# Modulation sums of a two-layer encoder: from float32 products to float32r halves

## The chip, the cores and the metric

The kernel runs on one core of one Trainium2 chip. The metric is the device time of one execution in microseconds (us). The engines are named as in the profile: PE is TensorE (matrix products), PEld its weight loads, DVE is VectorE, ACT is ScalarE, POOL is GpSimd, SP is SyncE, whose queue here issues nearly all transfers.

## The reference

Two layers over 256 positions of width 2048. In each, a vector c gives six modulation vectors of 2048; the mixers' bodies are left out here.

```python
c_act = jax.nn.silu(c)
for l in range(DEPTH):
    mod = (c_act @ w_mod[l] + b_mod[l]).reshape(bn, 6, d)
    shift_m, scale_m, gate_m = mod[:, 0, None], mod[:, 1, None], mod[:, 2, None]
    shift_f, scale_f, gate_f = mod[:, 3, None], mod[:, 4, None], mod[:, 5, None]

    h = layer_norm(x) * (1.0 + scale_m) + shift_m
    proj = h @ w_in[l]
    ...
    y = jnp.concatenate([y_a, y_b, y_c, y_d], axis=-1) @ w_out[l]
    x = layer_norm(ALPHA * x + (1.0 + gate_m) * y, post_mix_g[l], post_mix_b[l])

    h = layer_norm(x) * (1.0 + scale_f) + shift_f
    y = conv_ffn(h, ffn_w_up[l], ffn_w_conv[l], ffn_b_conv[l], ffn_w_down[l])
    x = layer_norm(ALPHA * x + (1.0 + gate_f) * y, post_ffn_g[l], post_ffn_b[l])
return x
```

## The kernel before

Most products are float32r products of halves. A weight tile `wraw` (128x2048) is loaded by SP's queue and split in two pieces of 128x1024 (`weights`, L368): ACT casts the high half `whi` (L403), DVE subtracts it from the raw tile for the low half `wlo` (L404). The activations are split in the same way (`split`, L420). TensorE sums high by high, high by low and low by high. The pool `splitp` holds four `whi` and four `wlo` tiles; each is taken again when the products that read it are done. In the first stages of layer 0 the weights are used as plain float32 (`wexact`, L379); these tiles come from the same pool.

The modulation vectors are made beside all this by `mod_stream` (L265). For each of the sixteen row blocks of `w_mod` it loads a tile `wmod`, and DVE adds it, times that block's entry of silu(c), to an accumulator `macc` of 128x2048 (L211). What is left is the sum over the 128 partitions. `settle` (L258) does that when the next vector is under way:

- `gate_rows` (L244) is for the two gates of a layer. They are needed along the free axis, the same in every partition: `ones` (128x128) is the stationary operand, 512 columns of `macc` the moving one, in float32, four times. ACT evicts each (`gate`, L251). The bias was added to one row of `macc` before.
- `mod_cols` (L190) is for shift and scale, which are needed along the partitions: for each block of 128 columns `macc` is the stationary operand and one column of `ones` the moving one, so there are sixteen products of one column, after one that puts the bias there. ACT evicts sixteen columns.

The order on each engine is made by a scheduler when the program is built; the source order and the pools' releases are what it starts from. `pump` (L321) spreads the steps of `mod_stream` over the units of weights. `out_proj` (L554) is the output projection (`o` in the profile) and the FFN's down projection (`d`). It goes over the columns in three chunks; at the end of each, `finish` multiplies the result by the gate row on DVE (`yg`, L586), adds it to the residual (`x`, L587) and takes statistics (L590): for the first chunk, of 1024 columns, four times three operations. `g_c` and `v_c` are the gate and value halves of the FFN's up projection, `C_c` is a float32 part of layer 0's input projection.

Of the kernel before, what the change touches and what calls it, by code (L numbers as in the profile page):

```python
# [7 lines left out]
F32 = mybir.dt.float32  # L8
F32R = mybir.dt.float32r
AF = mybir.ActivationFunctionType  # L10
ALU = mybir.AluOpType
AX = mybir.AxisListType

P = 128
# [4 lines left out]
KT = D // P  # L19
# [12 lines left out]
SHIFT_M, SCALE_M, GATE_M, SHIFT_F, SCALE_F, GATE_F = range(6)  # L32
# [22 lines left out]
def encoder_kernel(ctx: ExitStack, tc: tile.TileContext, A: dict, consts: bass.AP, out: bass.AP):  # L55
    nc = tc.nc
    pe, act, dve, pool = nc.tensor, nc.scalar, nc.vector, nc.gpsimd

    keep = ctx.enter_context(tc.tile_pool(name="keep", bufs=1))
    rawp = ctx.enter_context(tc.tile_pool(name="rawp", bufs=4))  # L60
    splitp = ctx.enter_context(tc.tile_pool(name="splitp", bufs=4))
# [11 lines left out]
    def tmp_tile(name):  # L73
        return tmpp.tile([P, 512], F32, tag="tmp", name=name)

    def ms_tile(name):
        return msp.tile([P, 512], F32, tag="ms", name=name)
# [4 lines left out]
    def mm(o, lhsT, rhs, start, stop):  # L82
        pe.matmul(o, lhsT, rhs, start=start, stop=stop, skip_group_check=True)  # L83

    def ident_act(o, i, scale, bias):
        return act.activation(out=o, in_=i, func=AF.Identity, scale=scale, bias=bias)
# [7 lines left out]
    ident = cst[:, 0:128]  # L94
# [2 lines left out]
    rotdup = cst[0:64, 384:512]  # L97
    cosT = cst[:, 512:768]
    sinT = cst[:, 768:1024]
    ones = keep.tile([P, P], F32, name="ones")  # L100
    pool.memset(ones, 1.0)
    mhalf = keep.tile([P, 4], F32, name="mhalf")
    pool.memset(mhalf, -0.5)

# [40 lines left out]
    bcol = []  # L145
# [40 lines left out]
    MOD, MOD_BY = {}, {}  # L186
# [3 lines left out]
    def mod_cols(l, m, k0, acc):  # L190

        n = acc.shape[1] // P
        ps = ms_tile("ps_mod")
        mm(ps[:, 0:n], ident, bcol[l][:, m * KT + k0 : m * KT + k0 + n], True, False)
        for j in range(n):
            mm(ps[:, j : j + 1], acc[:, j * P : (j + 1) * P], ones[:, 0:1], False, True)
        cols = keep.tile([P, n], F32, name=f"mod_{l}_{m}_{k0}")
        if m in (SHIFT_M, SHIFT_F):
            done = act.copy(cols, ps[:, 0:n])
        else:  # L200
            done = ident_act(cols, ps[:, 0:n], 1.0, ones[:, 0:1])
        for j in range(n):
            MOD[(l, m, k0 + j)] = cols[:, j : j + 1]
            MOD_BY[(l, m, k0 + j)] = done.ins.name

    def mod_step(acc, w, kt, first):
        col = cact[:, kt : kt + 1]
        if first:
            i = dve.tensor_scalar(out=acc, in0=w, scalar1=col, scalar2=None, op0=ALU.mult)
        else:  # L210
            i = dve.scalar_tensor_tensor(out=acc, in0=w, scalar=col, in1=acc, op0=ALU.mult, op1=ALU.add)  # L211
        held(i, "mod")

    def mod_piece(l, ms, k0, nkt):


        n, width = len(ms), nkt * P
        nk = 2048 // (n * width)
        acc = tmpp.tile([P, D], F32, tag="macc", name="qacc", bufs=2)[:, : n * width]
        units = []  # L220

        def unit(u):
            raw = raw_tile("wmod").rearrange("p (k m c) -> p k m c", k=nk, m=n)
            for i, m in enumerate(ms):
                c0 = m * D + k0 * P
                nc.sync.dma_start(
                    out=raw[:, :, i, :],
                    in_=A["w_mod"][l, u * nk * P : (u + 1) * nk * P, c0 : c0 + width].rearrange(
                        "(k p) c -> p k c", p=P
                    ),  # L230
                )
            for k in range(nk):
                mod_step(acc, raw[:, k, :, :].rearrange("p m c -> p (m c)"), u * nk + k, u == 0 and k == 0)

        for u in range(KT // nk):
            units.append(lambda u=u: unit(u))

        def sums():
            for i, m in enumerate(ms):
                mod_cols(l, m, k0, acc[:, i * width : (i + 1) * width])  # L240

        return units, sums

    def gate_rows(l, m, acc):  # L244

        g = keep.tile([P, D], F32, tag="gate", name=f"gate_{l}_{m}")
        for q in range(4):
            c = slice(q * 512, (q + 1) * 512)
            ps = ms_tile("ps_gate")
            mm(ps, ones, acc[:, c], True, True)  # L250
            ident_act(g[:, c], ps, 1.0, ones[:, 0:1])  # L251
        GATE[(l, m)] = g

    GATE = {}
# [3 lines left out]
    def settle(i=0):  # L258
        l, m, acc, k0, k1 = late.pop(i)
        if m in (GATE_M, GATE_F):  # L260
            gate_rows(l, m, acc)
        else:
            mod_cols(l, m, k0, acc[:, k0 * P : k1 * P])

    def mod_stream(order):  # L265
# [4 lines left out]
        for l, m in order:  # L270
            if (l, m) == (0, GATE_F):

                for u in range(4):
                    for v, acc in held_back.items():
                        raw = raw_tile("wmod").rearrange("p (k c) -> p k c", k=4)
                        nc.sync.dma_start(
                            out=raw,
                            in_=A["w_mod"][0, 4 * u * P : 4 * (u + 1) * P, v * D + LATE_KT * P : (v + 1) * D].rearrange(
                                "(k p) c -> p k c", p=P
                            ),  # L280
                        )
                        for k in range(4):
                            mod_step(acc[:, LATE_KT * P :], raw[:, k, :], 4 * u + k, u + k == 0)
                        if u == 3:
                            late.append((0, v, acc, LATE_KT, KT))
                        yield
            while len(late) >= 2:
                if late[0][:2] in WITH_NORM:
                    yield
                else:  # L290
                    settle()
# [5 lines left out]
            for kt in range(KT):  # L297
                raw = raw_tile("wmod")
                nc.sync.dma_start(out=raw[:, :w], in_=A["w_mod"][l, kt * P : (kt + 1) * P, m * D : m * D + w])
                if kt == KT - 1 and m in (GATE_M, GATE_F):  # L300
                    row = raw_tile("brow")
                    nc.sync.dma_start(out=row[0:1, :], in_=A["b_mod"][l : l + 1, m * D : (m + 1) * D])
                mod_step(acc[:, :w], raw[:, :w], kt, kt == 0)
                if kt == KT - 1:
                    if m in (GATE_M, GATE_F):
                        dve.tensor_tensor(out=acc[0:1, :], in0=acc[0:1, :], in1=row[0:1, :], op=ALU.add)
                    late.append((l, m, acc, 0, k1))
                yield
                if kt == 1 and late and late[0][:2] not in WITH_NORM:
                    settle()  # L310
# [16 lines left out]
    def need(l, m, k1=KT):  # L327
        while (l, m, k1 - 1) not in MOD and (l, m) not in GATE:
            at = [i for i, x in enumerate(late) if x[:2] == (l, m) and x[4] == k1]
            if at:  # L330
                settle(at[0])
            else:
                assert next(mods, "end") != "end"
# [25 lines left out]
    def held(i, kind):  # L359

        name, n = hold[kind]
        if n > 0:
            hold[kind][1] = n - 1
            tc.add_manual_dep(i.ins, name, order_dep, reason="the norm is what the next products wait for")
# [55 lines left out]
    def split(dst, src):  # L420
        hi, lo = dst[:2]
        act.copy(hi, src)  # L422
        dve.tensor_tensor(out=lo, in0=src, in1=hi.bitcast(F32), op=ALU.subtract)  # L423
# [970 lines left out]
def build(inputs):  # L1394
    import numpy as np
    import concourse.bacc as bacc

    nc = bacc.Bacc("TRN2", target_bir_lowering=False, num_devices=1)
    arrays, A = {}, {}
    for name in _INS:  # L1400
        a = np.ascontiguousarray(inputs[name])
        arrays[f"in_{name}_dram"] = a
        A[name] = nc.dram_tensor(f"in_{name}_dram", a.shape, mybir.dt.from_np(a.dtype), kind="ExternalInput").ap()
    c = _constants()
    arrays["in_consts_dram"] = c
    consts = nc.dram_tensor("in_consts_dram", c.shape, F32, kind="ExternalInput").ap()
    out = nc.dram_tensor("out_0_dram", (1, S, D), F32, kind="ExternalOutput").ap()
    with tile.TileContext(nc) as tc:
        encoder_kernel(tc, A, consts, out)
    return nc, arrays  # L1410
# [8 lines left out]
```

## Time and profile before

| what | value |
| --- | --- |
| three runs | 2348.81, 2357.82, 2362.06 us |
| median | 2357.82 us |
| span of the profiled execution | 2350.0 us |

For the profiled execution the page gives the span alone, no time of its own; the three runs are other executions. The span lies 1.2 us above the lowest of them and 7.8 below the median.

In the profile, a row such as "1525.44 3.87 PE L83 MATMUL ps_gate<-macc,ones ... x8" says that eight matmuls that began at line 83 started at 1525.44 us and were done 3.87 us later; L83 is the helper `mm`, so products are told apart by the names of their tiles. Matmuls are pipelined: their own lengths overlap, and what one costs in a stream is the distance of the starts.

### The profile page before, as it was taken

The page shows a single profiled execution, that of the slowest core. Times are in us where ns is not written, and L with a number is a line of the kernel's source. Part 1 is how long each engine was busy: PE and PEld are TensorE (multiplying, and loading weights), DVE is VectorE, ACT ScalarE, POOL GpSimd, SP SyncE. Part 2 cuts the span into 40 slices and gives each one's busy share as a digit, 9 for nine tenths or more (in the row PEclk, how much of TensorE's full clock was granted, in tenths as well). Part 3 has the DMA queues.
Part 4 walks back from the last instruction along what each step waited for, and adds up shares of the span by engine and source line. Part 5 has one row for each costly group of instructions (what it writes and reads, how often), then busy time and mean ns, then how long its engine had stood idle before and what let it go on. Part 6 is the DMA issues. An engine that isn't in the chain of part 4 may idle for free. (4 is left out here: it accounts for less than half of the span.)

```text
span 2350.0 us, 30996 instructions
## 1 busy us (share of the span) xinstructions
PE 2259.1 (96%) x12183; PEld 1924.6 (82%) x12183; DVE 1811.3 (77%) x2293; ACT 1036.4 (44%) x1478; POOL 38.0 (2%) x59
## 2 busy tenths in 40 slices
PE   6899999799999999999989999989999999999998
PEld 4688886498888888888878999867888888888786
DVE  6868987789888887988976986787676656665676
ACT  2221241345455544544535434435454455554553
POOL 2000000000000000000000000000000000000000
PEclk9899999899999999999998999999999999999999
DMA  9999779498889898898756566856767655556554
GB/s 338 368 316 329 285 274 383 159 341 309 308 312 329 291 327 296 309 328 294 274 186 228 191 227 199 297 185 233 236 234 247 205 190 181 193 183 197 179 197 144
DMA packets 226491, 605.17 MB, mean 258 GB/s; under 512 B 14484, under 2 KB 27012, under 8 KB 208676
## 3 DMA queue, kind: packets, MB, share of 16 engines
q1 hardware_dynamic: 225560, 602.29, 73.2%
q8 instruction: 95, 1.56, 0.3%
q0 software_dynamic: 784, 0.90, 0.1%
q14 instruction: 52, 0.43, 0.0%
HBM read 601.05 MB, written 2.10 MB: 257 GB/s over the span
## 5 line engine op out<-in xcount | busy, mean ns | idle before, releaser
L404 DVE TENSOR_TENSOR wlo<-wraw,whi 128x1024 fp32r<-128x1024 f32 (+1 forms) x645 | 775.7, 1216 | 360.4 <-ACT whi L403 354.5
L403 ACT CAST whi<-wraw 128x1024 fp32r<-128x1024 f32 (+1 forms) x645 | 670.9, 1046 | 817.8 <-PE g_c L83 208.2
L83 PE MATMUL v_c<-hT,whi 128*128 128x512 f32 x1344 | 473.1, 397 | 0.0
L83 PE MATMUL g_c<-hT,whi 128*128 128x512 f32 x1272 | 450.3, 398 | 0.0
L83 PE MATMUL d<-whi,a 128*128 128x512 f32 x1344 | 388.4, 391 | 0.3 <-ACT whi L403 0.3
L211 DVE SCALAR_TENSOR_TENSOR macc<-wmod,cact,macc 128x2048 f32<-128x2048 f32 (+2 forms) x180 | 358.1, 1993 | 38.9 <-DMA wmod<-in_w_mod_dram 38.2
L83 PE MATMUL v_c<-hT,wlo 128*128 128x256 f32 x1344 | 376.9, 281 | 0.0
L83 PE MATMUL g_c<-hT,wlo 128*128 128x256 f32 x1272 | 358.2, 282 | 0.0
L83 PEld LDWEIGHTS v_c<-hT,whi 128*128 128x128 f32 x1344 | 252.3, 188 | 60.1
L83 PEld LDWEIGHTS d<-whi,a 128*128 128x128 f32 x1344 | 252.9, 188 | 53.7 <-ACT whi L403 0.8
L83 PEld LDWEIGHTS g_c<-hT,whi 128*128 128x128 f32 x1272 | 239.7, 188 | 57.4 <-issue 0.5
L83 PEld LDWEIGHTS v_c<-hT,wlo 128*128 128x128 f32 x1344 | 254.0, 189 | 0.3 <-DVE wlo L404 0.2
L83 PEld LDWEIGHTS g_c<-hT,wlo 128*128 128x128 f32 x1272 | 241.4, 190 | 0.7 <-issue 0.5
L83 PE MATMUL d<-wlo,a 128*128 128x512 f32 x672 | 234.4, 391 | 0.8 <-DVE wlo L404 0.8
L83 PEld LDWEIGHTS d<-wlo,a 128*128 128x128 f32 x672 | 126.6, 188 | 27.6 <-DVE wlo L404 1.1
L83 PE MATMUL o<-whi,a 128*128 128x512 f32 x352 | 99.6, 392 | 0.1
L708 DVE SCALAR_TENSOR_TENSOR convD<-gluD,pm,convD 128x245 f32<-128x245 f32 (+23 forms) x240 | 98.7, 467 | 0.5
L423 DVE TENSOR_TENSOR a<-g,a 128x512 fp32r<-128x512 f32 x132 | 89.0, 686 | 0.0
L83 PE MATMUL D_c<-hT,whi 128*128 128x256 f32 x432 | 83.9, 294 | 2.5 <-ACT hT L422 2.0
L422 ACT CAST a<-g 128x512 fp32r<-128x512 f32 x132 | 81.3, 616 | 7.2 <-PE d L83 6.0
L211 DVE SCALAR_TENSOR_TENSOR qacc<-wmod,cact,qacc 128x1024 f32<-128x1024 f32 (+1 forms) x75 | 80.3, 1070 | 2.6 <-DMA wmod<-in_w_mod_dram 0.5
L83 PEld LDWEIGHTS o<-whi,a 128*128 128x128 f32 x352 | 66.0, 188 | 14.4 <-ACT whi L403 0.5
(310 smaller groups left out, 2667.4 us busy)
## 6 DMA issues: line engine op xcount, KB each, us to landing
wraw<-in_ffn_w_up_dram SPq DMA_DIRECT2D x176, 1024.0 KB, 5.4
wmod<-in_w_mod_dram SPq DMA_DIRECT2D x136, 1024.0 KB, 5.7
wraw<-in_ffn_w_down_dram SPq DMA_DIRECT2D x88, 1024.0 KB, 5.2
wraw<-in_w_in_dram SPq DMA_DIRECT2D x34, 1024.0 KB, 5.9
wmod<-in_w_mod_dram SPq DMA_DIRECT2D x64, 512.0 KB, 8.0
wmod<-in_w_mod_dram SPq DMA_DIRECT2D x32, 768.0 KB, 6.8
wraw<-in_w_out_dram SPq DMA_DIRECT2D x24, 1024.0 KB, 7.3
wexact<-in_w_in_dram SPq DMA_DIRECT2D x44, 512.0 KB, 6.5
```

Of the source, the lines that this page charges most:

```text
L83: pe.matmul(o, lhsT, rhs, start=start, stop=stop, skip_group_check=True)
L211: i = dve.scalar_tensor_tensor(out=acc, in0=w, scalar=col, in1=acc, op0=ALU.mult, op1=ALU.add)
L403: act.copy(hi[:, :m], r)
L404: i = dve.tensor_tensor(out=lo[:, :m], in0=r, in1=hi[:, :m].bitcast(F32), op=ALU.subtract)
L422: act.copy(hi, src)
L423: dve.tensor_tensor(out=lo, in0=src, in1=hi.bitcast(F32), op=ALU.subtract)
L708: dve.scalar_tensor_tensor(out=yd[:, j, 30 - k :], in0=glu[:, j, : S - 30 + k], scalar=CW(k, j), in1=yd[:, j, 30 - k :], op0=ALU.mult, op1 ...
```

## The change

The sums over the partitions of six vectors (the gates of both layers, and layer 1's SHIFT_F and SCALE_F) are no longer float32 products. `macc` is split in halves first, `mhi` by a cast on ACT and `mlo` by a subtraction on DVE, in two pieces of 128x1024, whose tiles come from the ring of the weight halves. A gate is then eight float32r products, high and low for each of four blocks of 512 columns. For SHIFT_F and SCALE_F of layer 1 the new function `mod_rows` uses stationary operands of four columns, of which one is ones: so block j of 512 columns lands in row j of one PSUM bank. That is copied (`mrow`), turned by four transposes, and DVE adds the bias (and 1 for the scale). The other shifts and scales stay as they were. `ones` becomes a view of the new tile `onesR`, which is cast on ACT at the start.

```diff
-    ones = keep.tile([P, P], F32, name="ones")
-    pool.memset(ones, 1.0)
+    flat = tmp_tile("flat")
+    pool.memset(flat[:, 0:P], 1.0)
+    pool.memset(flat[:, P : P + 16], 0.0)
+    for j in range(4):
+        pool.memset(flat[:, P + 5 * j : P + 5 * j + 1], 1.0)
+    onesR = keep.tile([P, P + 16], F32R, name="onesR")
+    act.copy(onesR, flat[:, : P + 16])
+    ones = onesR[:, 0:P].bitcast(F32)
...
+    def halves(acc, c0):
+        hi = splitp.tile([P, 1024], F32R, tag="whi", name="mhi")
+        lo = splitp.tile([P, 1024], F32R, tag="wlo", name="mlo")
+        split((hi, lo), acc[:, c0 : c0 + 1024])
+        return [(hi[:, i * 512 : (i + 1) * 512], lo[:, i * 512 : (i + 1) * 512]) for i in range(2)]
+
+    def mod_rows(l, m, acc):
+
+        ps = ms_tile("ps_row")
+        for j, pair in enumerate(halves(acc, 0) + halves(acc, 1024)):
+            for n, part in enumerate(pair):
+                mm(ps[0:4, :], onesR[:, P + 4 * j : P + 4 * j + 4], part, j + n == 0, j + n == 4)
+        row = tmp_tile("mrow")
+        act.copy(row[0:4, :], ps[0:4, :])
+        ps = ms_tile("ps_mod")
+        for i in range(4):
+            pe.transpose(ps[:, 4 * i : 4 * i + 4], row[0:4, i * P : (i + 1) * P], ident[0:4, 0:4])
+        cols = keep.tile([P, KT], F32, name=f"mod_{l}_{m}")
+        done = dve.scalar_tensor_tensor(
+            out=cols.rearrange("p (i j) -> p i j", i=4),
+            in0=ps[:, 0:KT].rearrange("p (i j) -> p i j", i=4),
+            scalar=0.0 if m == SHIFT_F else 1.0,
+            in1=bcol[l][:, m * KT : (m + 1) * KT].rearrange("p (j i) -> p i j", i=4),
+            op0=ALU.add,
+            op1=ALU.add,
+        )
...
-        for q in range(4):
-            c = slice(q * 512, (q + 1) * 512)
-            ps = ms_tile("ps_gate")
-            mm(ps, ones, acc[:, c], True, True)
-            ident_act(g[:, c], ps, 1.0, ones[:, 0:1])
+        for h in range(2):
+            for i, (hi, lo) in enumerate(halves(acc, h * 1024)):
+                c0 = h * 1024 + i * 512
+                ps = ms_tile("ps_gate")
+                mm(ps, onesR[:, 0:P], hi, True, False)
+                mm(ps, onesR[:, 0:P], lo, False, True)
+                ident_act(g[:, c0 : c0 + 512], ps, 1.0, ones[:, 0:1])
...
+        elif (l, m) in ((1, SHIFT_F), (1, SCALE_F)):
+            mod_rows(l, m, acc)
```

How the orders differ is shown at three places. A row holds its number on that engine, the line of the program, the operation with its tiles, the shape, and how often it stands in a row.

VectorE at layer 1's GATE_F, in the FFN's down projection (`d`; `x_88` and `x_89`, later `x_95` and `x_96`, are the two halves of the residual; `a<-g,a` are low halves of activations). Before:

```order
1535 L404 TENSOR_TENSOR wlo<-wraw,whi 128x1024 x2
1536 L423 TENSOR_TENSOR a<-g,a 128x2x256
1537 L404 TENSOR_TENSOR wlo<-wraw,whi 128x1024 x2
1538 L586 TENSOR_TENSOR yg<-d_000_17175,gate_5_17983 128x512
1539 L586 TENSOR_TENSOR yg<-d_001_17176,gate_5_17983 128x512
1540 L587 SCALAR_TENSOR_TENSOR x_88<-x_88,yg 128x512 x2
1541 L590 BN_STATS st_d_17147<-x_88 128x6 x2
1542 L586 TENSOR_TENSOR yg<-d_010_17177,gate_5_17983 128x512
1543 L586 TENSOR_TENSOR yg<-d_011_17178,gate_5_17983 128x512
1544 L587 SCALAR_TENSOR_TENSOR x_89<-x_89,yg 128x512 x2
1545 L590 BN_STATS st_d_17148<-x_89 128x6 x2
1546 L404 TENSOR_TENSOR wlo<-wraw,whi 128x1024 x2
```

And now:

```order
1545 L464 TENSOR_TENSOR a<-g,a 128x2x256
1546 L464 TENSOR_TENSOR mlo<-macc,mhi 128x1024 x2
1547 L445 TENSOR_TENSOR wlo<-wraw,whi 128x1024
1548 L627 TENSOR_TENSOR yg<-d_000_17230,gate_5_18038 128x512
1549 L627 TENSOR_TENSOR yg<-d_001_17231,gate_5_18038 128x512
1550 L628 SCALAR_TENSOR_TENSOR x_95<-x_95,yg 128x512 x2
1551 L631 BN_STATS st_d_17202<-x_95 128x6 x2
1552 L627 TENSOR_TENSOR yg<-d_010_17232,gate_5_18038 128x512
1553 L627 TENSOR_TENSOR yg<-d_011_17233,gate_5_18038 128x512
1554 L628 SCALAR_TENSOR_TENSOR x_96<-x_96,yg 128x512 x2
1555 L631 BN_STATS st_d_17203<-x_96 128x6 x2
1556 L445 TENSOR_TENSOR wlo<-wraw,whi 128x1024 x4
```

Before, the pair of low halves of the next unit of weights stood ahead of the twelve residual operations. Now the two `mlo` and one `wlo` stand there, and the second `wlo` of that unit is the first of the four behind them.

TensorE at the same gate, from the end of the first chunk's products (`d_010`, `d_011`) into the second chunk (`d_102400`). Before:

```order
9328 L83 MATMUL d_010_17177<-whi,a 128x512
9329 L83 MATMUL d_011_17178<-whi,a 128x512
9330 L83 MATMUL ps_gate<-macc,ones 128x512 x3
9331 L83 MATMUL d_102400_18028<-whi,a 128x512
9332 L83 MATMUL ps_gate<-macc,ones 128x512
9333 L83 MATMUL d_102400_18028<-wlo,a 128x512
9334 L83 MATMUL d_102400_18028<-whi,a 128x512 x2
```

And now:

```order
9360 L83 MATMUL d_010_17232<-whi,a 128x512
9361 L83 MATMUL d_011_17233<-whi,a 128x512
9362 L83 MATMUL ps_gate<-mhi,onesR 128x512 x2
9363 L83 MATMUL d_102400_18095<-whi,a 128x512
9364 L83 MATMUL d_102400_18095<-wlo,a 128x512
9365 L83 MATMUL d_102400_18095<-whi,a 128x512
9366 L83 MATMUL ps_gate<-mlo,onesR 128x512 x2
9367 L83 MATMUL d_102400_18095<-whi,a 128x512
9368 L83 MATMUL d_102400_18095<-wlo,a 128x512
9369 L83 MATMUL d_102400_18095<-whi,a 128x512 x2
9370 L83 MATMUL d_102400_18095<-wlo,a 128x512
9371 L83 MATMUL ps_gate<-mhi,onesR 128x512
```

Four rows of float32 (each shown as two instructions in the profile) have become eight, with the high and low products of a block apart and products of the next chunk in between.

SyncE's queue ahead of layer 0's GATE_M, where the last float32 weights of the input projection (`wexact`) are loaded. Before:

```order
75 L381 DMA wexact<-in_w_in_dram 128x1024
76 L299 DMA wmod<-in_w_mod_dram 128x1536 x2
77 L381 DMA wexact<-in_w_in_dram 128x1024 x2
78 L299 DMA wmod<-in_w_mod_dram 128x1536 x2
79 L381 DMA wexact<-in_w_in_dram 128x1024 x2
80 L299 DMA wmod<-in_w_mod_dram 128x1536 x3
81 L381 DMA wexact<-in_w_in_dram 128x1024 x2
82 L389 DMA wraw<-in_w_out_dram 128x2x1024
```

And now:

```order
75 L422 DMA wexact<-in_w_in_dram 128x1024
76 L340 DMA wmod<-in_w_mod_dram 128x1536 x2
77 L422 DMA wexact<-in_w_in_dram 128x1024 x2
78 L340 DMA wmod<-in_w_mod_dram 128x1536 x5
79 L430 DMA wraw<-in_w_out_dram 128x2x1024
80 L340 DMA wmod<-in_w_mod_dram 128x1536 x2
81 L430 DMA wraw<-in_w_out_dram 128x2x1024
82 L422 DMA wexact<-in_w_in_dram 128x1024
83 L340 DMA wmod<-in_w_mod_dram 128x1536
84 L422 DMA wexact<-in_w_in_dram 128x1024 x3
85 L340 DMA wmod<-in_w_mod_dram 128x1536
```

The last four loads of `wexact` stood as one pair ahead of three `wmod` and a second pair behind them, both ahead of the output projection's first `wraw`. Now they stand behind the first two `wraw`: one, then a `wmod`, then three together.

More of the change, by code (lines that the diff above doesn't have):

```diff
@@ L204, in mod_cols @@
             MOD_BY[(l, m, k0 + j)] = done.ins.name
+    def halves(acc, c0):
[22 more added lines that the diff above has]
+        )
+        for k in range(KT):
+            at = 4 * (k % 4) + k // 4
+            MOD[(l, m, k)] = cols[:, at : at + 1]
+            MOD_BY[(l, m, k)] = done.ins.name
     def mod_step(acc, w, kt, first):
```

## The prediction

> **What bounds the kernel now.** I read the page first, then TensorE's waits, then the chain of waits, then the single stretches that the change touches.
>
> ```profile
> span 2350.0 us, 30996 instructions
> PE 2259.1 (96%) x12183; PEld 1924.6 (82%) x12183; DVE 1811.3 (77%) x2293; ACT 1036.4 (44%) x1478; POOL 38.0 (2%) x59
> PE   6899999799999999999989999989999999999998
> ```
>
> TensorE is busy for 96% of the span. The dips are at the start, in slice 8 and where a LayerNorm stands. VectorE is the next engine with 77%, so there is room on it on average, but not in every place.
>
> ```profile
> PE ps_xT L535 <- ACT xn L86: 36.5, 10, 7.8
> PE ps_xT L1241 <- ACT xn L86: 14.0, 2, 13.7
> PE D_c L83 <- DVE wlo L404: 3.4, 2, 2.6
> ```
>
> These are the longest waits of TensorE (total, number of times, longest). The first two are norms; the change does not touch them. In the streams of out projection and FFN, where five of the six changed sums stand, TensorE hardly waits at all. So there a microsecond taken from TensorE is a microsecond of the span, as long as the next weight halves arrive that much earlier too. That last condition decides this case.
>
> **The four gates.** What a gate costs now is seen in the chain (start, length, what), at layer 1's GATE_F:
>
> ```profile
> 2214.99 1.72 PE ps_gate L83 x4
> ...
> 2216.71 1.13 PE ps_gate L83 x2
> 2217.84 0.23 PE d L83
> 2218.07 0.87 PE ps_gate L83 x2
> 2218.93 9.09 PE d L83 x40
> ```
>
> Its eight instructions (each of the four float32 products shows as two) take 1.72 + 1.13 + 0.87 = 3.72 us. The last row has the price of a float32r product of 512 columns: 9.09 / 40 = 0.227 us. The new gate is eight of those, 1.81 us if it flows. So a gate frees **1.9 us** of TensorE. What it costs elsewhere are two casts on ScalarE and two subtractions on VectorE, of the same 128x1024 shape as the weight halves:
>
> ```profile
> L404 DVE TENSOR_TENSOR wlo<-wraw,whi 128x1024 fp32r<-128x1024 f32 (+1 forms) x645 | 775.7, 1216 | 360.4 <-ACT whi L403 354.5
> L403 ACT CAST whi<-wraw 128x1024 fp32r<-128x1024 f32 (+1 forms) x645 | 670.9, 1046 | 817.8 <-PE g_c L83 208.2
> ```
>
> That is 2.1 us of ScalarE and 2.4 us of VectorE for each sum. ScalarE waits 817.8 us for its inputs over the span, so its share is hidden. VectorE's is not hidden everywhere, so each gate is worked out at its place.
>
> Layer 1, GATE_M (first out projection chunk; start, length, what):
>
> ```profile
> 1525.44 3.87 PE L83 MATMUL ps_gate<-macc,ones 128*128 128x512 f32 x8
> 1526.43 1.22 DVE L404 TENSOR_TENSOR wlo<-wraw,whi 128x1024 fp32r<-128x1024 f32 x1
> 1527.56 1.28 DVE L586 TENSOR_TENSOR yg<-o,gate 128x512 f32<-128x512 f32 x2
> ...
> 1533.55 1.28 DVE L590 BATCH_NORM_STATS2 st_o<-x 128x6 f32<-128x512 f32 x2
> 1534.74 2.35 DVE L404 TENSOR_TENSOR wlo<-wraw,whi 128x1024 fp32r<-128x1024 f32 x2
> ```
>
> Twelve operations of the residual (yg, x, bn_stats) take 7.2 us on VectorE, from 1527.56 to 1534.74, and the next low half stands behind them. In the changed order mlo, mlo and one wlo come first, from 1526.43: three of 1.2 us end at 1530.0, the twelve end at 1537.2, and the second wlo (call it wlo b) at 1538.4. TensorE's product that reads wlo b is the 47th instruction from the gate's first one; 46 x 0.227 = 10.4 us after 1525.44, that is 1535.9. So TensorE would stand **2.5 us** for it: 1.9 won, 2.5 lost, +0.6 us.
>
> Layer 1, GATE_F (the same place of the FFN's down projection):
>
> ```profile
> 2213.66 1.06 ACT L403 CAST whi<-wraw 128x1024 fp32r<-128x1024 f32 x1 [2.51 <-PE d L83]
> 2214.74 2.58 DVE L404 TENSOR_TENSOR wlo<-wraw,whi 128x1024 fp32r<-128x1024 f32 x2 [2.25 <-ACT whi L403]
> 2217.24 1.28 DVE L586 TENSOR_TENSOR yg<-d,gate 128x512 f32<-128x512 f32 x2
> 2223.22 1.28 DVE L590 BATCH_NORM_STATS2 st_d<-x 128x6 f32<-128x512 f32 x2
> 2224.42 2.35 DVE L404 TENSOR_TENSOR wlo<-wraw,whi 128x1024 fp32r<-128x1024 f32 x2
> ```
>
> Here both wlo stand ahead of the twelve operations now; in the changed order the two mlo take their places, wlo a follows, and wlo b goes behind the twelve. VectorE is idle before 2214.74. The cast that stands at 2213.66 becomes the first mhi. From 2214.74 on: mlo to 2215.9, the second (its cast ends at 2216.1) to 2217.2, wlo a to 2218.4, the twelve (7.2 us) to 2225.6, wlo b to 2226.7. The gate starts at about 2214.8; wlo b is the 47th again, 10.4 us later, and some 0.4 us are lost inside the gate where its evictions wait behind a cast of ScalarE: 2225.6. A stand of 1.1 us: 1.9 - 0.4 - 1.1 = **0.4 us won**.
>
> Layer 0, GATE_F lies in an up projection without residual operations behind it:
>
> ```profile
> 653.34 2.92 PE L83 MATMUL ps_gate<-macc,ones 128*128 128x512 f32 x6
> ```
>
> The last two of its eight instructions come after two other products, and it costs the same 3.7 us. The low-half gate products are put about 14 instructions behind the high-half ones, 14 x 0.227 = 3.2 us, against 2.4 us of mlo. I count the whole **1.9 us**.
>
> Layer 0, GATE_M lies in the stage with plain float32 weights, which share the ring of tiles (L379) with the new halves:
>
> ```profile
> 284.84 2.06 SPq L381 DMA_DIRECT2D wexact<-in_w_in_dram  x2
> 295.03 2.06 SPq L381 DMA_DIRECT2D wexact<-in_w_in_dram  x2
> 306.66 3.79 PE L83 MATMUL ps_gate<-macc,ones 128*128 128x512 f32 x8
> 310.28 12.04 PE L83 MATMUL C_c<-hF,wexact 128*128 128x256 f32 x55
> wexact<-in_w_in_dram SPq DMA_DIRECT2D x44, 512.0 KB, 6.5
> ```
>
> The mhi and mlo take four of the eight tiles, so the last four loads of wexact on SyncE's queue, issued at 284.84 and 295.03 now, wait for products just ahead of the gate and for the gate itself: they issue at 306 to 309. With 6.5 us to landing that gives 312.5 to 315.5. TensorE reaches the first of them after a gate of 1.8 us and 16 C_c products of 12.04 / 55 = 0.219 us: 306.7 + 1.8 + 3.5 = 312. So it stands 0.5 to 3.5 us, less what a quicker landing gives back; I take 1.6 and 0.3 inside the gate, which leaves **0** (bounds -1.6 and +2).
>
> **The two sums of shift and scale.** Layer 1's SHIFT_F and SCALE_F now:
>
> ```profile
> 790.32 3.71 PE L83 MATMUL ps_mod<-ones,macc 128*128 128x1 f32 x32
> 921.55 0.29 PE L83 MATMUL ps_mod<-bcol,cst 128*128 128x16 f32 x2
> 921.69 3.76 PE L83 MATMUL ps_mod<-ones,macc 128*128 128x1 f32 x32
> 925.31 0.78 PE L83 MATMUL g_c<-hT,whi 128*128 128x512 f32 x1
> 926.10 0.63 PE L83 MATMUL g_c<-hT,whi 128*128 128x512 f32 x1
> 928.65 0.39 PE L83 MATMUL g_c<-hT,whi 128*128 128x512 f32 x1
> 279.64 0.38 PE L973 MATMUL ps_pT<-cst,p 128*128 128x128 f32 x2
> ```
>
> From 921.55 to 925.31 are 3.76 us for 34 instructions, and the other sum takes the same. In their place come eight products of 512 columns, 1.81 us, and four small transposes. No transpose of four rows is in the trace; the nearest are the ps_pT, two in 0.21 us by their starts, so 0.1 each. Below, they could cost next to nothing; above, 0.23 like a full product. I take 0.1, 0.4 in all: 2.2 us against 3.76. Waits for the first mhi or mrow I put at 0.3, since other products stand between mrow's copy and its transposes. So **1.2 us** each, 2.4 for both (bounds 0 and 3.5). The halves run beside up projections, with two wlo and a macc step per unit on VectorE; the bias addition and mrow's copy are one operation each, needed only at the norm at 1569.
>
> **The clock.** The rows from 925.31 show more: five pairs of g_c products (a whi and a wlo) take 3.34 us, up to 928.65. In a whole unit from the chain, the first row below, a pair takes 22.61 / 64 = 0.35 us, five 1.77. The windows (behind the busy times the granted clock, then DMA) name the reason:
>
> ```profile
> 1643.02 22.61 PE g_c L83 x128
> 795.00:800.00 5.00, 5.00 (x31) 4.43 (x30) 0.66 (x1) 1.40 (x2) 0.00 (x0) 1.00 0.85 311
> 920.00:925.00 5.00, 5.00 (x42) 4.80 (x41) 4.14 (x8) 2.65 (x4) 0.00 (x0) 1.00 0.58 203
> 925.00:930.00 5.00, 5.00 (x22) 4.34 (x22) 2.29 (x2) 0.28 (x1) 0.00 (x0) 0.66 0.96 317
> ```
>
> The clock was 0.66 on average just behind the narrow products, and the five pairs lost 3.34 - 1.77, about **1.5 us**. The same stretch at 790.32 was followed by none of this: 1.00 in the window from 795. With dense products in its place I expect that the drop at 925 goes.
>
> [...]
>
> **Start.** One small cast, one more table load and five more memsets stand ahead of the modulation vector. The first modulation step waits for its weights, so I count 0 (bounds 0 and 1.3).
>
> **The sum.** +0.6 - 0.4 - 1.9 + 0 - 2.4 - 1.5 + 0 = **-5.6 us**, -0.24%. It is made against the span of 2350.0 us; the runs were 2348.81 to 2362.06 with a median of 2357.82, and I take the difference to the median: **2352 us**. About 0.5% (11.8 us) is what a measurement of this kernel can tell from no change.
>
> **Rivals.**
>
> *All of it is won.* The waits that I put at the out projections and at wexact do not come about, because VectorE catches up: 4 x 1.9 + 2 x 1.5 + 1.5 = 12.1 us, 2345.7 us, -0.51%. For it: VectorE's 77%, and 46 products are a long cover. Against it: the order puts wlo b behind the twelve operations by name, and the row at 1534.74 shows that even now it ends at 1535.9, just when it is needed. Chance 0.15.
>
> *The halves hold up the ring.* The mechanism: mhi and mlo take two of four whi and two of four wlo tiles, so the unit of weights behind a sum can be cast only when the sum has read its halves. If at a sum a cast and a subtraction (1.05 + 1.22 = 2.27 us) come late for both tiles of that unit, TensorE stands 4.5 us: a gate then loses 2.6 us and a folded sum 3.0 (4.5 less 1.5). At all six, 4 x 2.6 + 2 x 3.0 = 16.4 us less the 1.5 of the clock: about +15, 2373 us. Half of it at all places, or all at three, is near +6. It decides where the first mhi is cast later than 2.3 us ahead of its first product. For it: the casts' idle time is mostly ended by TensorE's release (208.2 us of it by g_c). Against it: at 2213.66 the cast that becomes mhi ends before the gate starts. Chance 0.12.
>
> *The clock drops elsewhere.* The gates save, but a stretch of narrow or waiting work that escaped now is caught (a later modulation sum, or the stand for wlo b): 1.5 us back for each, two of them +3. Then about -3, 2355 us. Chance 0.13; inside "no change".
>
> **The numbers.** Forecast -5.6 and its neighbourhood (-1 to -10): 0.6. Faster by over 0.5%: the first rival, and a little of the forecast's edge: 0.17. Slower by over 0.5%: most of the second rival: 0.10. Within: 0.73. The range reaches from 2343 (the full gain, and a few us for the spread of the runs around their median) to 2363 (half of the ring's price).
>
> **What will show it.** ps_gate should be 32 products of about 0.39 us in the list by tile, ps_row 16, and their stretches near 2 us. wlo b behind the first twelve residual operations of each layer 1 projection should be named as what o and d wait for, 2.5 and 1.1 us. The loads of wexact should issue near 306. The window at 925 should show a clock of 1.00. I am wrong if TensorE waits for mhi, mlo or whi by more than a microsecond at the up projections, or if ScalarE's order delays something that I left out.

## The result and the profile after

The changed kernel took 2351.69 us (median of 22 runs, 2338.61 to 2357.93), the kernel before 2357.47 us beside it (22 runs, 2343.77 to 2363.85). The ratio is 0.9973 with a 95% interval of 0.9961 to 0.9986: 3 to 9 us faster. The median's 5.8 us lie beside the forecast 5.6, well inside what was called no change.

The two profiled executions say the opposite at first sight. The page of the changed kernel:

```profile
span 2354.4 us, 30941 instructions
PE 2258.3 (96%) x12139; PEld 1921.4 (82%) x12139; DVE 1824.5 (77%) x2307; ACT 1049.6 (45%) x1492; POOL 38.2 (2%) x64
```

Its span is 4.4 us longer than that of before. That is the first thing to learn here: runs of the same program differ by 20 us, so two single profiles compare sites, not totals. The list by tile gives the new products (least, median and longest in ns), and the waits of TensorE those that the prediction named:

```profile
L83 PE MATMUL ps_gate<-mlo,onesR x16: 389/395/496, 310.6 to 2223.5; 128*128 128x512 f32 x16
L83 PE MATMUL ps_row<-mlo,onesR x8: 388/392/398, 797.5 to 930.1; 128*4 128x512 f32 x8
PE o L83 <- DVE wlo L445: 2.2, 1, 2.2
PE d L83 <- DVE wlo L445: 1.8, 2, 1.1
PE o L83 <- ACT whi L444: 0.9, 1, 0.9
```

Products and both predicted waits are there. (Of the two waits of d, the one of 1.1 us is the predicted one; the other, 0.8 us at 1209, stood in the kernel before as well, at 1205.) At layer 1's GATE_M, VectorE and then TensorE:

```profile
1527.83 2.35 DVE L248 SCALAR_TENSOR_TENSOR macc<-wmod,cact,macc 128x2048 f32<-128x2048 f32 x1 [2.18 <-DMA wmod<-in_w_mod_dram]
1530.10 2.36 DVE L464 TENSOR_TENSOR mlo<-macc,mhi 128x1024 fp32r<-128x1024 f32 x2
1532.48 1.22 DVE L445 TENSOR_TENSOR wlo<-wraw,whi 128x1024 fp32r<-128x1024 f32 x1
1533.62 1.28 DVE L627 TENSOR_TENSOR yg<-o,gate 128x512 f32<-128x512 f32 x2
...
1539.61 1.28 DVE L631 BATCH_NORM_STATS2 st_o<-x 128x6 f32<-128x512 f32 x2
1540.81 3.48 DVE L445 TENSOR_TENSOR wlo<-wraw,whi 128x1024 fp32r<-128x1024 f32 x3
1528.58 0.68 PE L83 MATMUL ps_gate<-mhi,onesR 128*128 128x512 f32 x2
1542.07 0.50 PE L83 MATMUL o<-wlo,a 128*128 128x512 f32 x1 [2.23 <-DVE wlo L445]
```

The order is the predicted one: two mlo, one wlo, twelve residual operations, then the second wlo, for which TensorE stands 2.23 us (2.5 were forecast). At layer 1's GATE_F and at the place of the old clock drop:

```profile
2231.52 0.50 PE L83 MATMUL d<-wlo,a 128*128 128x512 f32 x1 [1.05 <-DVE wlo L445]
925.00:930.00 5.00, 5.00 (x28) 3.55 (x27) 4.12 (x8) 3.69 (x5) 0.00 (x0) 1.00 0.62 222
```

A stand of 1.05 us (1.1 were forecast), and a clock of 1.00 at 925.

To compare sites I took the start of the same product (the k-th of a tile's name) in two traces, and the difference of the two starts ahead of a site and behind it. What the difference grows by is what the site costs against the first profile of before. The table anticipates the experiments, whose kernels follow; all is in us.

| site | change | change again | gates only | rows only | before again | forecast |
| --- | --- | --- | --- | --- | --- | --- |
| layer 0 GATE_M (262 to 320) | -0.8 | -1.7 | -1.5 | 0.0 | +0.8 | 0 |
| layer 0 GATE_F (645 to 669) | -1.7 | -1.7 | -1.8 | 0.0 | -0.1 | -1.9 |
| first folded sum (785 to 801) | -1.2 | -1.2 | +3.4 | -1.3 | +1.6 | -1.2 |
| second folded sum (918 to 935) | -2.8 | -2.8 | +1.6 | -2.8 | -0.1 | -1.2 - 1.5 |
| layer 1 GATE_M (1512 to 1546) | +1.3 | +2.2 | +0.6 | 0.0 | 0.0 | +0.6 |
| layer 1 GATE_F (2210 to 2235) | -0.2 | -0.2 | -0.2 | 0.0 | 0.0 | -0.4 |

### The profile page after: what moved, and what is told of

The parts are those of the page before. It is cut to its first block, busy times and chain, and to the rows that moved or that the text cites. A ratio compares the mean times of both kernels' runs of the same rounds, so it can differ in the third digit from the quotient of the medians.

```text
span 2354.4 us, 30941 instructions
## 1 busy us (share of the span) xinstructions
PE 2258.3 (96%) x12139; PEld 1921.4 (82%) x12139; DVE 1824.5 (77%) x2307; ACT 1049.6 (45%) x1492; POOL 38.2 (2%) x64
```

## The experiments

**The same two programs, profiled again.** No edit.

> The kernel before, unchanged, profiled a second time. In its first profile the up projection of layer 0 ran at 353 ns per pair of a 512-column and a 256-column product up to the gate at 653, at 347 ns from there to 921, and at 353 ns again afterwards, and the clock dropped at 925. If pace and clock drops belong to the execution (the phase of a window that the program doesn't set), the places differ this time: another share of the 2500 or so pairs at 347 ns, and a span up to 17 us away from 2350 (2500 x 0.0067). If they belong to the program (the float32 gate and the narrow products set them), 653 to 921 is fast again, 925 drops again, and the span is within 2 us of 2350.

> The changed kernel, unchanged, profiled a second time. In its first profile all pairs of the up projections ran at 353 ns, and the clock dropped at 243 and at 1380 beside the norms. If that belongs to the execution, a fast stretch or other drops appear this time and the span moves by several us from 2354.4; if the change itself keeps the pace slow, all pairs are at 353 ns again. What the sites themselves give or take must be the same in both: about -1.8 us over layer 0's GATE_F, -1.3 over the first folded sum, +1.3 over layer 1's GATE_M, within 0.3 us.

Spans: 2347.9 us and 2348.5 us, so the changed kernel's span moved by 5.9 us between two of its own executions. The windows (busy TensorE and its instructions, granted clock, DMA share, GB/s) of before again, then of the change again:

```profile
560.00:640.00 80.00, 80.00 (x463) 1.00 0.87 312
790.00:800.00 10.00, 10.00 (x53) 0.83 0.63 249
920.00:935.00 15.00, 15.00 (x91) 0.89 0.53 180
```

```profile
790.00:800.00 10.00, 10.00 (x57) 1.00 0.77 278
920.00:935.00 15.00, 15.00 (x85) 1.00 0.62 225
```

Where the clock fell it stood at 0.50: in the first profile of before from 925.3 to 928.5. A mean of 0.83 over 10 us is then 3.4 us at half rate. So before again has a drop behind both narrow sums, where the first profile had one, at 921; the change has none in either profile. The pace of the up projections moved too: the first profile of before has 455 instructions between 560 and 640, this one 463 in the same 80 us. Counted over the run in stretches of twelve pairs, 732 pairs were at 347 ns in the first and 1104 in the second, of some 2500; in the two profiles of the change one stretch of twelve each. The sites of the change repeat, but for +2.2 at layer 1's GATE_M: there the clock dropped right at the stand for wlo b, from 1536 on. So clock drops and pace differ between two executions of one program. The drops have an order in the traces: within each profile all half-rate windows begin whole multiples of 3.413 us apart, to within 0.01 us, and this grid lies elsewhere against the program in each execution (its first point is 0.20 us behind the span's start in the first profile of before, 1.20 in that of the change).

**Layer 1's gates earlier.**

```diff
             def load(u, c0=c0, width=width, nk=nk, units=units, last=last):
+                if l == 1 and c0 == 0 and u == units - 2:
+                    box["gate"] = gate_of()
...
-                if c0 == 0:
+                if c0 == 0 and l == 0:
                     box["gate"] = gate_of()
```

> The changed kernel with layer 1's two gates summed two units of weights earlier, so that their mlo and both wlo of the unit behind the chunk stand ahead of the twelve residual operations on VectorE. By the queue theory the waits of o for wlo (2.2 us) and of d for wlo (1.8 us) in the list of TensorE's waits go below 0.3 us each, and the path over these two gates is 2.5 and 1.1 us shorter than in the changed kernel: about -1.2 and -1.3 us against the kernel before. By the rival (it is the ring: the halves take tiles from the weights wherever they are made) a wait for whi or wlo of about the same 2 us turns up at the earlier place, and nothing is won.

Measured: 2346.66 us in its one run. From 1500, ahead of the earlier gate, to 1546 it won 0.8 us against before (1.2 were expected), where the change loses 1.3; over GATE_F it won 1.3, as expected. No wait of o for wlo is left; one of d is, 0.7 us, but at 1092 and not at the gate. TensorE's list has these instead:

```profile
PE o L83 <- ACT whi L444: 0.6, 1, 0.6
PE ps_gate L83 <- ACT mhi L463: 0.6, 1, 0.6
```

The second stands at the earlier GATE_M. So the queue theory holds, and the ring rival has a share of half a microsecond, not of two.

**Layer 1's gates in float32.**

```diff
+        if l == 1:
+            for q in range(4):
+                c = slice(q * 512, (q + 1) * 512)
+                ps = ms_tile("ps_gate")
+                mm(ps, ones, acc[:, c], True, True)
+                ident_act(g[:, c], ps, 1.0, ones[:, 0:1])
+            GATE[(l, m)] = g
+            return
```

> The changed kernel with layer 1's two gates as float32 products of macc again, without halves there. Against the kernel before, the path over layer 1's GATE_M is the same again (0 within 0.3 us, where the change had +1.3) and over GATE_F too (where it had -0.2). The waits of o and d for wlo are as before, 0 to 1 us. If the +1.3 comes from something else that the change shifted in time (the phase of modulation steps against the chunk), it stays.

Measured: 0.0 over both gates, 2355.45 us in its one run. The loss at GATE_M belongs to the halves of that gate.

**One half of the change each.** Rows only puts the condition of the edit above to `True`; gates only leaves out the `elif` that calls `mod_rows`.

> Only layer 1's SHIFT_F and SCALE_F summed from halves; all four gates are float32 products of macc as before. My account: -1.3 us at each of the two sums from shorter products, and another 1.5 us at each wherever the kernel before has a clock drop behind it (three of four such places in two profiles of it), so -4 to -5 us against the kernel before, about 0.998, if nothing else moves. No clock drop behind the two sums; layer 1's GATE_M as before. Rival: the sums are worth nothing in the whole because the drop of the clock comes at another place; then 1.000 and as many drops as before. The pace of layer 0's up projection (347 ns a pair in parts of both profiles before, 353 in all four of changed kernels): if the gates' form decides it, fast stretches are back here.

> Only the four gates summed from halves; SHIFT_F and SCALE_F of layer 1 by sixteen narrow products as before. My account: -1.7 at layer 0's GATE_F, -0.8 at its GATE_M, +1.3 and -0.2 in layer 1, +1 at the start, so about -0.5 us and a ratio of 1.000; clock drops behind the narrow sums at some 790 and 920 are back, at one or both. Rival (the gates carry the gain, the folded sums little): 0.998. If the gates' form decides the pace of layer 0's up projection, it is 353 ns a pair throughout.

Measured against the same runs of before: rows only 0.9976 (0.9951 to 1.0001), gates only 0.9999 (0.9975 to 1.0023). The two intervals overlap, so the times alone don't part them; the sites do (table above). In gates only the drops are back at both sums, twice as long:

```profile
790.00:800.00 10.00, 10.00 (x52) 0.66 0.85 315
920.00:935.00 15.00, 15.00 (x84) 0.80 0.85 302
```

0.66 over 10 us is 6.8 us at half clock, which cost 3.4 us at this site. The gates alone win 2.9 us at their four sites, and the whole shows nothing of it. Both have stretches at 347 ns a pair: 624 pairs in rows only, up to the first folded sum at 794 and not behind it; 408 in gates only, of which the larger part ends at layer 0's GATE_F.

**What sets the pace.** Two tries: another order of the products, and other addresses (`onesR` as `[P, P + 64]`).

```diff
                         mm(o, hi[:, off], both.rearrange("p h t -> p (h t)"), kt == 0, False)
+                    for i in part:
+                        o = box["c"][i]
+                        off = slice(i * P, (i + 1) * P)
                         mm(o[:, :S], lo[:, off], both[:, 0, :], False, kt == KT - 1)
```

> The changed kernel with the up projections' products in another order: for each row block the two 512-column products of whi, then the two 256-column products of wlo, in place of whi, wlo, whi, wlo; the sums are the same. If the two paces (347 and 353 ns a pair) come from how a 512-column product and a 256-column one meet, all four products in this order take 693 or another figure that doesn't switch within the run; 693 everywhere would make the span 15 us shorter than with 353. If the pace belongs to the execution, it is 353 or 347 ns a pair again, whatever the order.

> The changed kernel with onesR 48 columns wider, so that all tiles allocated behind it lie at addresses 256 bytes above those of the kernel before, where the change had shifted them by 64; nothing else differs. If addresses decide the pace of the up projections, there are stretches at 347 ns a pair as in both profiles before; if not, 353 throughout as in four profiles of changed kernels, or a mixture that chance deals. The sites are as in the changed kernel within 0.3 us.

The shifted tiles changed nothing: no more than twelve pairs at 347 ns, 2354.02 us, sites as in the change. The order of the products did. Windows of the change first, then of the change with two of whi and two of wlo:

```profile
1650.00:1760.00 110.00, 110.00 (x625) 1.00 0.71 242
```

```profile
1650.00:1760.00 110.00, 110.00 (x634) 1.00 0.70 249
```

634 instructions in 110 us are 347 ns a pair, 625 are 352. Layer 1 ran at 353 ns in all nine profiles with the old order up to here, but for at most 12 pairs; with the new one it ran 6.5 us shorter (from 1640 to 2100), and all of layer 0's pairs were fast as well.

**The order on both kernels, and everything together.** The first is the kernel before with the order alone; the second is the change with it; the third is the change with the earlier gates and this at the start; the last has all.

```diff
-    act.copy(onesR, flat[:, : P + 16])
+    dve.tensor_copy(onesR, flat[:, : P + 16])
```

> The kernel before with the up projections' products ordered as two of whi, then two of wlo, and nothing of the change. All pairs at 347 ns, where the two profiles before had 1764 and 1368 of some 2500 at 353: 9 to 12 us less than the kernel before, 0.995 to 0.996. The clock drops behind the two narrow sums are there at some of the places. If the order helps only together with the change, it is 1.000.

> The changed kernel with the same order of the up projections' products, timed. Beside the kernel before in that order the pace is the same in both, so what is left is the change without it: by the sites -1.7 (layer 0's GATE_M), -1.7 (GATE_F), -1.25 twice (folded sums), +0.6 and -0.2 (layer 1's gates), +0.4 (a wait for whi at 375): -5.1, and -1.6 for each clock drop behind a narrow sum that is spared (three of four in the profiles): -7 to -8. Against the kernel before: 0.992 to 0.993. By the rival account (the narrow sums' clock drops only move) the difference is -5, 0.994.

> The changed kernel with layer 1's gates summed two units earlier and onesR cast on VectorE, so that ScalarE loads no extra table at the start. Against the kernel before the 5.8 us of the change, 1.4 more at layer 1's GATE_M, 1.1 at GATE_F, 0 to 1 at the start: -8 to -9, 0.996 to 0.997. If the loss at layer 1's gates was only a matter of phase, 0.9975 as the change.

> Both together: the changed kernel with layer 1's gates earlier, onesR cast on VectorE, and the up projections' products as two of whi, then two of wlo. All pairs at 347 ns; no wait of o for wlo; against the kernel before -17 to -20 us, 0.991 to 0.993, the fastest of all. If one of the parts disturbs another, it is no faster than the order alone with the change.

| kernel | median (lowest to highest), runs | ratio to before (95%) |
| --- | --- | --- |
| before, new order | 2350.89 (2345.90 to 2354.76), 12 | 0.9979 (0.9961 to 0.9996) |
| change, new order | 2341.05 (2336.11 to 2344.91), 6 | 0.9928 (0.9903 to 0.9953) |
| change, earlier gates, start | 2349.32 (2337.85 to 2357.03), 12 | 0.9968 (0.9947 to 0.9989) |
| all of it | 2340.64 (2337.05 to 2341.89), 6 | 0.9925 (0.9902 to 0.9949) |

With the new order all pairs are fast with the change and without it, and the spread of the runs is about 9 us for both where it had been 20. The two ranges do not overlap, and the medians lie **9.8 us** apart: that is the change without the lottery of the pace, more than the 7 to 8 expected. The windows of before in the new order show more than the one drop that the forecast had:

```profile
790.00:800.00 10.00, 10.00 (x46) 0.66 0.66 258
920.00:935.00 15.00, 15.00 (x92) 0.89 0.67 242
```

Drops at both sums again, 6.8 and 3.4 us at half clock. Site by site from the one profile to the other: GATE_M -1.7, GATE_F -1.9, first sum -4.5, second -2.8, layer 1 +0.4 and -0.2, together -10.7. Yet the spans of the two profiles, 2344.9 and 2339.6 us, are only 5.3 us apart: outside the sites the changed kernel lost 5.4 us in its profile. Of that, twice 1.7 us are clock drops behind two short stretches of one-column products that both kernels have, at 239 (20 instructions) and at 416 (24 instructions, 2.6 us). Before in the new order, then the change in it:

```profile
412.00:427.00 15.00, 15.00 (x54) 1.00 0.54 206
```

```profile
412.00:427.00 15.00, 15.00 (x50) 0.89 0.65 245
```

In the fourteen profiles the first of these stretches was caught five times and the second nine times, always in a kernel with folded sums. That looks like a cost of the change, but the grid of 3.413 us tells the cases apart. Counted from a point of the grid, the first stretch was caught where it began from 3.33 on or up to 0.10 us, and never from 1.03 to 3.24; the second from 2.90 on or up to 1.05, and never from 1.59 to 2.79. So the execution deals these drops, and the profiles of the folded sums were unlucky there: one profile of each kernel can't confirm the 9.8 us, which rest on the runs.

The order alone gave less than expected (3 us, 0.9 to 9 by its interval, where I had 9 to 12): the two profiles of before are then no fair sample of its pace, or other waits took some of it; the runs don't tell which.

The earlier gates show at their sites in both kernels (no wait of o for wlo in either, -1.3 at GATE_F in both), but 2 us are below what these runs part: 0.9968 lies beside the change's 0.9973, and 2340.64 beside 2341.05. The fastest versions are the two with change and new order, 0.7% below before; what the earlier gates win is shown at their sites alone, not in the times.

## Why the prediction was right, point by point

- **The bound.** Right at the sites: what a site took from TensorE's path is found in the starts of the products behind it. Between the sites the starts move by as much again, by clock drops and pace.
- **Layer 0's GATE_F, 1.9.** Right in kind and size: 1.7.
- **The folded sums, 1.2 each.** Right: 1.2 to 1.3 without the clock, but for the version with everything, where TensorE waits 0.9 us for mlo at the first sum and 0.2 is left. The transposes that I bounded by 0 and 0.23 took 0.12 each:

```profile
932.06 0.41 PE L228 MATMUL ps_mod<-cst,mrow 4*128 4x4 f32 x4
```

- **Layer 1's GATE_M, +0.6.** Right: +0.6 in gates only, shown by the wait, by its going with earlier gates and by its absence with float32 gates. In the profile above it was +1.3, since a macc step that waited for its wmod held the first mlo until 1530.10, 1.5 us behind the gate's start, not 1.0. In two of the six profiles that sum this gate in halves at this place, the clock dropped at the stand (1536) and cost 1.6 more.
- **Layer 1's GATE_F, -0.4.** Right in kind; -0.2.
- **Layer 0's GATE_M, 0.** The step that failed: "So it stands 0.5 to 3.5 us, less what a quicker landing gives back; I take 1.6". No such wait is in the list, and the site won 1.5 to 1.75 in every profile but the first, which had 0.8 (without an edit the site moved by 0.8 between the two profiles of before, so a single figure is good to about a microsecond). SyncE's queue and TensorE in the profile after:

```profile
308.81 0.33 SPq L422 DMA_DIRECT2D wexact<-in_w_in_dram  x1
310.54 1.51 SPq L422 DMA_DIRECT2D wexact<-in_w_in_dram  x3
310.16 0.58 PE L83 MATMUL ps_gate<-mhi,onesR 128*128 128x512 f32 x1
313.22 5.13 PE L83 MATMUL C_c<-hF,wexact 128*128 128x256 f32 x23
```

  The issues were nearly as forecast: from 0.7 us ahead of the gate's start to 2.3 behind it by the prediction, from 1.4 ahead to 1.5 behind (the last of the three) in the trace. What was wrong is TensorE's way to the first of these tiles. The prediction counted 16 C_c products at 12.04 / 55 = 0.219 us, 3.5 us in all; but 0.219 is the price of one row, and each float32 product shows as two. In the trace 32 rows of C_c stand between the gate's start and the first product that waits for one of these loads: 4 within the gate and 28 behind it, 28 x 0.219 = 6.1 us. That product starts at 319.26, which is 9.1 us behind the gate's start and not 5.3. The other three loads landed at 317.4, 318.7 and 320.0, and TensorE needed them at 321.0, 327.9 and 329.6. With 7.0 in place of 3.5 the prediction's own sum gives 315.5, as late as its latest landing: no stand, and the whole 1.9 won but for the gaps inside the gate.
- **The clock, 1.5.** Right in kind, too small. I counted the one drop that the profile had. In four profiles with float32 sums there (before twice, gates only, before in the new order) seven of the eight places dropped, for ten windows of 3.4 us or 2.5 a run, some 3.9 us; in ten profiles with folded sums, none of twenty, though these sums began anywhere from 0.2 to 3.0 us behind a point of the grid. (A sum at 1098 that every kernel makes of one-column products was followed by a drop in 13 of the 14.) The 3.9 us are the gain at the two sums. Over the whole span the profiles with folded sums had no less time at half clock than the four others (104 us each on average), in part because of the unlucky stretches at 239 and 416. That the gain stays is shown by the runs in the new order, not by these totals. Why the clock falls is not shown: it did so behind seven of the eight float32 sums of 3.76 us, and behind the stretch of 2.6 us at 416 in nine of the fourteen profiles.
- **What I did not see: the pace.** With the old order of the products, all four profiles that keep float32 products at layer 0's gates or at the two sums had hundreds of fast pairs in layer 0 (732, 1104, 624, 408); of six profiles with both in halves, only one had more than 24 (264). So the change seems to give back part of its gain: some 900 pairs by 6.7 ns would be 6 us, if the two profiles of before were typical. The gap between 9.8 us at equal pace and the 5.8 of the result is 4 us. How often the runs without a profile were fast is not known, so the split is argued, not shown.
- **Start, 0, and a new wait.** The extra table load is seen, 1.28 us on ScalarE at 2.65 (TensorE waits 4.3 us for crow, 3.3 before), but the products at 45 to 60 stood within 1 us of before on either side in all kernels. A wait for whi at 375 of 0 to 1.1 us was not in the sum.

That the total came out within 0.2 us is luck. The prediction had 1.7 too little at layer 0's GATE_M and 2.4 too little for the clock, which makes 4.1 us too little; what made up for them, as far as the runs tell, is a pace that I did not know. Of the rivals, *the clock drops elsewhere* had a part, at 1536 by the new stand for wlo b and at 239 and 416 by chance. *The halves hold up the ring* showed only as waits of 0.6 to 0.9 us, nowhere near the 4.5 us that it needed at a sum. *All of it is won* fell with the waits for wlo b.

## What to carry to other kernels

On a kernel bound by one engine, price a saving at its place: here 1.9 us became 1.7 where the helping engine was free, and -0.6 where twelve operations stood in its queue behind the new ones. Look for what else a stretch of narrow products costs: here the clock drops behind them cost more (3.9 us a run) than the shorter products saved (2.4). And where runs of one program spread by 20 us, profile it more than once before reading a total, and find what spreads them; its removal can be worth as much as the change (here an order of four products took 6.5 us from layer 1 alone).

## What the runs showed of the hardware

- Alternating float32r products of 512 and 256 columns ran at one of two paces, 347 or 353 ns a pair, for hundreds of pairs at a stretch. In the first profile of before the pace switched at the gate at 653 and at the sum at 921 (455 instructions in the 80 us from 560, 636 in the 110 us from 670). Two of 512 and then two of 256 ran at 347 to 348 throughout, in four profiles. Both paces were seen on each of the two chips that ran the experiments. Why is open; a shift of addresses by 192 bytes more made no difference in its one run.
- Behind a stretch of 3.6 to 4.6 us of one-column float32 products the clock fell to half for one or two windows of 3.4 us in 20 of 22 places; behind the same sums as 512-column products it did in none of 20, even with four-column weights.
- The half-rate windows of a run lie on a grid of 3.413 us. Whether a stretch of one-column products of 2.6 us was followed by a drop went with its place in that grid (9 of 14 and 5 of 14 places, 1.7 us each), and the two misses of the longer stretches began 1.46 and 1.63 us behind a point of the grid, where the nearest that were caught began at 1.06 and 1.82.
